# Inverting the delta rule's unit triangles: 32-blocks by substitution in place, instead of 16-blocks joined by products

## Chip, cores and metric

One core of a Trainium2 chip runs the whole kernel in one launch. The time is device microseconds of one execution. The engines are named as the profile names them: PE (TensorE, matmuls), DVE (VectorE), ACT (ScalarE), POOL (GpSimd) and SP (SyncE, which here only issues DMA transfers).

## The reference

Four layers run one after the other on 256 rows of width 1024: two attention layers, then two layers of a mixer followed by a gated feed-forward. The mixer has three branches, and one of them is the gated delta rule in chunks of 64 rows, with 4 heads:

```python
k_beta = k * beta[..., None]
m = jnp.where(strict, jnp.einsum('bhnid,bhnjd->bhnij', k_beta, k) * decay, 0.0)
a = m + jnp.eye(CHUNK, dtype=m.dtype)
rhs = jnp.concatenate([v * beta[..., None], k_beta * jnp.exp(G)[..., None]], axis=-1)
sol = lax.linalg.triangular_solve(a, rhs, left_side=True, lower=True, unit_diagonal=True)
u, w = sol[..., :dv], sol[..., dv:]
...
def step(state, inp):
    v_new = u_c - jnp.einsum('bhck,bhkv->bhcv', w_c, state)
    o = jnp.einsum('bhck,bhkv->bhcv', qd_c, state) + jnp.einsum('bhcj,bhjv->bhcv', a_c, v_new)
    state = state * dl_c[..., None, None] + jnp.einsum('bhck,bhcv->bhkv', kt_c, v_new)
```

What the change touches is the inverse of `a`, a unit lower triangle of 64 x 64 for each chunk and head (16 of them a layer).

## The kernel before

Rows lie on the 128 partitions, in two tiles `tt` of 128 rows (two chunks each). Every dense product runs on weights that are streamed in pieces: `piece` (line 423) loads a piece into a `raw` slot, ACT rounds it to `whi`, DVE forms the rest `wlo`, and `mm3` makes three matmuls of it. Between the dense products stand the small steps of attention or of the mixer.

The order is not written by hand. All operations are recorded first (`record`, line 237), with the boxes of the tiles that they read and write; overlapping boxes make dependencies. A planner (`schedule`, line 303) then goes through time with a cost for each operation and, on each engine, takes the earliest recorded one that is ready; `emit` (line 381) writes the instructions out in that order, so in the profile nearly all carry line 391. Tiles come from classes with a fixed number of slots (12 of `b`, 8 of `s`, 5 PSUM slots of `sd`, 4 of `raw`, 7 each of `whi` and `wlo`), given out in the order in which the tiles were recorded. A box is narrowed by an index only as long as the tile was not rearranged: a view made by `rearrange` keeps the whole box it had (`LA`, line 114).

The mixer (line 940) computes the strict triangle `M` per row tile and head (line 1183) and inverts `I + M` in three stages:

1. The solve (lines 1213 to 1228). `d16` masks the 16-blocks of the diagonal, a reduction packs them into `cN`, and eight small transfers bring each block into one partition of `Nb` (64 blocks on 64 partitions). Fifteen steps of a multiply and a subtract then build the inverse of each block in `Tb`. Eight transfers bring them back into `cT` (line 1231), all eight writing a rearranged view.
2. The expansion (lines 1232 to 1238): `Tm` sets the blocks on the diagonal, and DVE transposes them into `Sm`. `level4` (line 1242) joins pairs of 16-blocks to 32-blocks: per row tile four products of `M` and `Sm`, a mask, four products of `Tm` and the result, a subtraction, then small transposes into `Te`.
3. `level5` (line 1257) joins 32-blocks to 64-blocks in the same way, on 64-wide tiles.

`uu` and `wq` (line 1298) follow, then the state loop over four chunks (line 1317), the output and its branch product. In the recorded order the solve stands behind half 0 of the pool branch, and then come gate and branch products, the convolutions of v and q (`qkv`, line 1127), `vb` and `kb`; `level4` is called after half 0 of the retention branch and before `qkv(0)`, `level5` after the scores `attnT`.

Of the kernel before, what the change touches and what calls it, by code (L numbers as in the profile page):

```python
# [12 lines left out]
AF = mybir.ActivationFunctionType  # L13
ALU = mybir.AluOpType
AX = mybir.AxisListType

P = 128
S = 256
# [13 lines left out]
def rope_np(pos, dim):  # L32
    inv = np.float32(10000.0) ** (-np.arange(0, dim, 2, dtype=np.float32) / np.float32(dim))
    ang = pos.astype(np.float32)[:, None] * inv.astype(np.float32)[None, :]
    ang = np.concatenate([ang, ang], axis=-1).astype(np.float64)
    sgn = np.concatenate([-np.ones(dim // 2), np.ones(dim // 2)])
    return np.cos(ang), np.sin(ang) * sgn[None, :]


def tok(a):  # L40
    return a.reshape(2, P, -1).transpose(1, 0, 2).reshape(P, -1)


def constants():
    t = np.arange(S)
    rc, rs = rope_np(t // 64, 32)
    cc, cs = rope_np(t % 64, 32)
    cosA, sinA = np.concatenate([rc, cc], 1), np.concatenate([rs, cs], 1)
    cosB, sinB = rope_np(t, 64)
    cosC, sinC = rope_np(t, 32)  # L50
    i = np.arange(P)
    ident = np.eye(P)
    m0 = np.where(i[None, :] <= i[:, None], 0.0, -1e30)
    mT0 = np.where(i[None, :] >= i[:, None], 0.0, -1e30)
    c1 = [ident, tok(cosA), tok(sinA), tok(cosB), tok(sinB), tok(cosC), tok(sinC), m0, mT0]
    same = (i[:, None] // 64) == (i[None, :] // 64)
    lt1 = (same & (i[:, None] <= i[None, :])).astype(float)
    ls = (same & (i[:, None] > i[None, :])).astype(float)
    r0 = np.repeat((i[:, None] < 64).astype(float), P, 1)
    r1 = 1.0 - r0  # L60
    masks = [((i[:, None] // 16) == (i[None, :] // 16)).astype(float)]
    for lv in range(4, 5):
        b = 2 ** lv
        masks.append((((i[:, None] // (2 * b)) == (i[None, :] // (2 * b)))
                      & ((i[None, :] // b) % 2 == 1) & ((i[:, None] // b) % 2 == 0)).astype(float))
    cosR, sinR = rope_np(t, 128)
    eye16 = np.tile(np.eye(16).reshape(1, 256), (P, 1))
    c2 = [lt1, ls, r0, r1, lt1.T] + masks + [tok(cosR), tok(sinR), eye16]
    gam = 1.0 - 2.0 ** (-5.0 - np.arange(4))
    jj, ii = t[:, None], t[None, :]  # L70
    ex = np.where((jj // 64) == (ii // 64), np.abs(ii - jj), ii - jj)
    dd = [np.where((jj // 64) <= (ii // 64), g ** np.maximum(ex, 0).astype(float), 0.0) * 128 ** -0.5 for g in gam]
    pc = []
    for w in (2, 4, 8, 16):
        pc.append(((jj <= ii) & (jj > ii - w)) / np.minimum(ii + 1.0, w) - (jj == ii))
    d0 = np.concatenate([a[:P] for a in dd], 1)
    d1 = np.concatenate([a[P:, P:] for a in dd], 1)
    p0 = np.concatenate([a[:P, :P + 16] for a in pc], 1)
    p1 = np.concatenate([a[P:, P:] for a in pc], 1)
    f = lambda l: np.ascontiguousarray(np.concatenate(l, 1).astype(np.float32))  # L80
    return {"k1": f(c1), "k2": f(c2), "kd0": f([d0]), "kd1": f([d1]), "kp0": f([p0]), "kp1": f([p1])}
# [312 lines left out]
class Net:  # L394
# [527 lines left out]


    def setup2(self):
        k2 = self.const("kk", [P, 1664], self.I["k2"])
        m = lambda i: k2[:, i * P:i * P + P]
        self.lt1, self.ls, self.r0, self.r1, self.li, self.m16 = (m(i) for i in range(6))
        self.mask4 = m(6)
        self.cosR = k2[:, 896:1152].rearrange("p (t d) -> p t d", t=2)
        self.sinR = k2[:, 1152:1408].rearrange("p (t d) -> p t d", t=2)  # L930
        self.eye16 = k2[:, 1408:1664].rearrange("p (r c) -> p r c", r=16)
        self.ones = self.nc.tile("c", [P, P])
        self.nc.vector.memset(self.ones, 1.0)
        self.lt1r = self.nc.tile("c", [P, P], F32R)
        self.nc.scalar.copy(self.lt1r, self.lt1)
# [4 lines left out]
    def mixer(self, l, xT, rx, nxt):  # L940
        nc = self.nc
# [53 lines left out]
        for h0 in (0, 2):  # L995
            ps = self.sd([P, 2, S])
# [3 lines left out]
        ps = self.sd([P, 4, P])  # L1000
# [10 lines left out]
        for tt in range(2):  # L1011
# [12 lines left out]
            r = self.rsqrt(mv[:, :, 1], 4, 1.0, GN_EPS)  # L1024
# [12 lines left out]
        for g0 in (0, 2):  # L1037
            ps = self.sd([P, 2, S])
# [4 lines left out]
            ps = self.sd([P, 2, S])  # L1043
# [25 lines left out]
        d = sm()  # L1069
# [14 lines left out]
        ps = self.sd([P, 4, 8])  # L1084
# [25 lines left out]
        for tt in range(2):  # L1110
# [3 lines left out]
            ps = self.sd([P, 4, P])  # L1114
# [50 lines left out]
        M = em  # L1165
        bhr, bGr = nc.tile("m", [P, 8]), nc.tile("m", [P, 8])
        for tt in range(2):
            h8 = slice(tt * 4, tt * 4 + 4)
            ps = self.sd([P, 4, P])
# [9 lines left out]
            r, r2 = self.tiny(4), self.tiny(4)  # L1179
# [30 lines left out]

        y = [self.b(12 + tt, [P, D]) for tt in range(2)]
        branch("w_branch_pool_2", 0, oT, 0, gate(1, 0), True)
        cp = self.b(0, [P, 832])
        cN, cT = (cp[:, i * P:i * P + P].rearrange("p (t h c) -> p t h c", t=2, h=4) for i in range(2))
        Nb, Tb = (cp[0:64, 320 + i * 256:576 + i * 256].rearrange("p (r c) -> p r c", r=16) for i in range(2))
        for tt in range(2):
            d16 = self.s2([P, 4, P])
            nc.vector.tensor_tensor(d16, M[:, tt], self.hb(self.m16), ALU.mult)
            nc.vector.tensor_reduce(cN[:, tt], d16.rearrange("p h (b c) -> p h c b", c=16), AX.X, ALU.add)
            for h in range(4):  # L1220
                nc.sync.dma_start(Nb[(tt * 4 + h) * 8:(tt * 4 + h) * 8 + 8], cN[:, tt, h])
        nc.vector.tensor_copy(Tb, self.eye16[0:64])
        for j in range(15):
            r, c = 15 - j, j + 1
            tmp = cp[0:64, 256:256 + r * c].rearrange("p (r c) -> p r c", r=r)
            nc.vector.tensor_tensor(tmp, Nb[:, c:16, j:j + 1].to_broadcast([64, r, c]),
                                    Tb[:, j:j + 1, 0:c].to_broadcast([64, r, c]), ALU.mult)
            nc.vector.tensor_tensor(Tb[:, c:16, 0:c], Tb[:, c:16, 0:c], tmp, ALU.subtract)
        for tt in range(2):
            for h in range(4):  # L1230
                nc.sync.dma_start(cT[:, tt, h], Tb[(tt * 4 + h) * 8:(tt * 4 + h) * 8 + 8])
        Tm, Sm = self.b(8, [P, 2, 4, P]), self.b(9, [P, 2, 4, P])
        for tt in range(2):
            nc.vector.tensor_tensor(Tm[:, tt].rearrange("p h (b c) -> p h b c", c=16),
                                    cT[:, tt].unsqueeze(2).to_broadcast([P, 4, 8, 16]),
                                    self.m16.rearrange("p (b c) -> p b c", c=16).unsqueeze(1).to_broadcast([P, 4, 8, 16]),
                                    ALU.mult)
            nc.vector.transpose(Sm[:, tt].rearrange("p h d -> p (h d)"), Tm[:, tt].rearrange("p h d -> p (h d)"))

        Te = [self.s2([64, 4, 64]) for tt in range(2)]  # L1240

        def level4():
            for tt in range(2):
                ps = self.sd([P, 4, P])
                for h in range(4):
                    nc.tensor.matmul(ps[:, h], M[:, tt, h], Sm[:, tt, h], start=True, stop=True)
                wt = self.s2([P, 4, P])
                nc.vector.tensor_tensor(wt, ps, self.hb(self.mask4), ALU.mult)
                ps = self.sd([P, 4, P])
                for h in range(4):  # L1250
                    nc.tensor.matmul(ps[:, h], Tm[:, tt, h], wt[:, h], start=True, stop=True)
                nc.vector.tensor_tensor(Sm[:, tt], Sm[:, tt], ps, ALU.subtract)
                for c in (0, 32):
                    nc.vector.transpose(Te[tt][c:c + 32, :, c:c + 32], Sm[2 * c:2 * c + 32, tt, :, 2 * c:2 * c + 32])
                    nc.gpsimd.memset(Te[tt][c:c + 32, :, 32 - c:64 - c], 0.0)

        def level5():
            v = lambda t: t.rearrange("p (c o r) -> p c o r", c=2, o=2)
# [22 lines left out]
        for tt in range(2):  # L1281
            nc.vector.tensor_tensor(kb[:, tt], kn[:, tt], hd(bGr, tt), ALU.mult)
        branch("w_branch_ret_2", 0, oT, 4, gate(2, 0), False)
        level4()
        qkv(0, qT)
        rqs = []
        for tt in range(2):
# [3 lines left out]
        for tt in range(2):  # L1291
            ps = self.sd([P, 4, P])
# [7 lines left out]
        for tt in range(2):  # L1300
            ps = self.sd([P, 4, P])
# [3 lines left out]
            ps = self.sd([P, 4, P])  # L1305
# [11 lines left out]
        for tt in range(2):  # L1317
            for c in range(2):
# [3 lines left out]
                if state is not None:  # L1322
                    ps = self.sd([P, 4, P])
# [4 lines left out]
                if (tt, c) != (1, 1):  # L1328
                    ps = self.sd([P, 4, P])
# [9 lines left out]
            ps = self.sd([P, 4, P])  # L1339
# [9 lines left out]
            r = self.rsqrt(ss, 4, 1.0 / P, EPS)  # L1349
# [136 lines left out]


CONST = constants()


# [16 lines left out]
```

## Time and profile before

| | |
|---|---|
| median of 3 runs | 1184.74 us (1184.53 to 1186.55) |
| profiled execution | 1184.63 us, its span 1182.9 us |
| PE busy | 1163.6 us, 98% |
| DVE busy | 875.9 us, 74% |
| ACT busy | 652.6 us, 55% |
| the mixers' solves on DVE | from 406 and from 866 us |

In a timeline each line is a start in us, a duration in us, the engine, the operation, its output and input tiles by class, shapes, and how many like it follow one another; a bracket gives the idle time before it and what ended that. Neighbouring matmuls and DVE instructions overlap, so the distance between two starts is less than a duration. A small f32 product shows as two matmuls.

### The profile page before, as it was taken

Reading aid. Unit: us, or ns where it says so; the run is one execution under the profiler, and the core shown is the slowest. Engines: PE = TensorE matmul, PEld = TensorE weight load, DVE = VectorE, ACT = ScalarE, POOL = GpSimd, SP = SyncE. Lnnn points to the kernel's source line nnn. Section 1 sums busy time; section 2 is a strip of 40 time slices with the busy share of each in tenths; the row PEclk is TensorE's granted clock in tenths of the full one; section 3 lists DMA queues with packets and bytes.
Section 4 is the critical chain, followed back from the end, with each engine's and each line's share of the span. In section 5 each row is a group of like instructions: output and inputs, shape, how many; then the busy total and the mean of one; then the engine's idle time right before and its main releaser. Section 6 shows DMA issues by size and latency. Waiting matters only on the chain.

```text
span 1182.9 us, 17313 instructions
## 1 busy us (share of the span) xinstructions
PE 1163.6 (98%) x6316; PEld 989.3 (84%) x6316; DVE 875.9 (74%) x1570; ACT 652.6 (55%) x1210; POOL 49.3 (4%) x73
## 2 busy tenths in 40 slices
PE   8999999999999999999999999999999999999997
PEld 6888898988898888788888888898888878888886
DVE  6899889997698886776565638679797777655643
ACT  6689678964465554465454436455545446544531
POOL 1100010000001000000000000000000101000000
PEclk9999999999999999999999999999999999999999
DMA  7444335645464664346644854544754354654651
GB/s 236 142 140 150 129 123 173 200 131 173 126 213 153 204 194 136 106 160 197 212 160 140 274 185 143 171 149 163 222 188 147 107 178 142 200 192 142 216 194 36
DMA packets 64662, 196.54 MB, mean 166 GB/s; under 512 B 11201, under 2 KB 12609, under 8 KB 64577
## 3 DMA queue, kind: packets, MB, share of 16 engines
q1 hardware_dynamic: 64576, 195.44, 51.0%
q8 instruction: 49, 0.80, 0.3%
q14 instruction: 37, 0.30, 0.1%
HBM read 194.10 MB, written 1.05 MB: 165 GB/s over the span
## 4 chain that ended last, share of the span: by engine, by line
PE 91%; DVE 5%; ACT 3%; issue 1%; POOLq 0%; DVEq 0%; ACTq 0%
PE acc L391 73%; PE sd L391 18%; DVE wlo L391 2%; DVE s L391 1%; DVE b L391 1%; ACT whi L391 1%; ACT s L391 1%; ACT tg L391 1%; ACT b L391 1%; ACT xh L391 1%; DVE ty L391 0%; DVE m L391 0%; DVE xl L391 0%; DVE tg L391 0%; DVE x L391 0%
## 5 line engine op out<-in xcount | busy, mean ns | idle before, releaser
L391 DVE TENSOR_TENSOR wlo<-raw,whi 128x1024 fp32r<-128x1024 f32 (+4 forms) x380 | 427.2, 1136 | 128.1 <-ACT whi L391 125.0
L391 ACT CAST whi<-raw 128x1024 fp32r<-128x1024 f32 (+4 forms) x380 | 369.2, 982 | 195.4 <-PE acc L391 141.2
L391 PE MATMUL acc<-whi,xh 128*128 128x512 f32 (+4 forms) x1184 | 445.5, 378 | 4.6 <-ACT whi L391 1.7
L391 PE MATMUL acc<-wlo,xh 128*128 128x512 f32 (+4 forms) x1184 | 442.3, 376 | 0.5 <-DVE wlo L391 0.5
L391 PE MATMUL acc<-whi,xl 128*128 128x512 f32 (+4 forms) x1184 | 441.6, 375 | 0.0
L391 PEld LDWEIGHTS acc<-whi,xh 128*128 128x128 f32 x1184 | 223.5, 189 | 42.6 <-ACT whi L391 2.4
L391 PEld LDWEIGHTS acc<-whi,xl 128*128 128x128 f32 x1184 | 223.8, 189 | 37.1 <-issue 0.4
L391 PEld LDWEIGHTS acc<-wlo,xh 128*128 128x128 f32 x1184 | 223.9, 189 | 36.5 <-DVE wlo L391 0.7
L391 PE MATMUL acc<-whi,b 128*128 128x512 f32 x328 | 107.5, 396 | 0.8 <-ACT b L391 0.8
L391 PEld LDWEIGHTS acc<-whi,b 128*128 128x128 f32 x328 | 61.5, 188 | 15.0 <-ACT b L391 1.1
L391 PE MATMUL sd<-b,b 128*128 128x128 f32 (+3 forms) x464 | 69.8, 288 | 0.0
L391 POOL TENSOR_TENSOR ty<-ty,m 128x4 f32<-128x4 f32 (+3 forms) x34 | 33.1, 978 | 852.7 <-DVE ty L391 852.7
L391 PE MATMUL acc<-wlo,b 128*128 128x512 f32 x164 | 64.9, 396 | 0.0
L391 PEld LDWEIGHTS sd<-b,b 128*128 128x128 f32 (+2 forms) x464 | 60.6, 190 | 4.3 <-DVE b L391 1.8
L391 ACT ACTIVATE b<-sd 128x512 fp32r<-128x512 f32 (+3 forms) x44 | 23.7, 538 | 63.1 <-PE sd L391 62.4
L391 ACT ACTIVATE s<-acc,r 128x512 f32<-128x512 f32 (+3 forms) x52 | 31.2, 600 | 47.0 <-PE acc L391 44.3
L391 PE MATMUL acc<-xh,whi 128*128 128x256 f32 x192 | 54.1, 282 | 0.0
L391 PE MATMUL acc<-xh,wlo 128*128 128x256 f32 x192 | 54.1, 282 | 0.0
L391 PE MATMUL acc<-xl,whi 128*128 128x256 f32 x192 | 53.9, 281 | 0.0
L391 PE MATMUL sd<-c,s 128*128 128x128 f32 (+2 forms) x268 | 42.6, 276 | 4.4 <-DVE s L391 2.8
L391 PEld LDWEIGHTS sd<-c,s 128*128 128x128 f32 (+2 forms) x268 | 32.4, 139 | 11.9 <-ACT b L391 3.3
L391 DVE SCALAR_TENSOR_TENSOR b<-sd,b 128x512 fp32r<-128x512 f32 (+3 forms) x44 | 26.9, 616 | 18.7 <-ACT b L391 17.8
(179 smaller groups left out, 1275.6 us busy)
## 6 DMA issues: line engine op xcount, KB each, us to landing
raw<-in_wt SPq DMA_DIRECT2D x308, 512.0 KB
raw<-in_wt SPq DMA_DIRECT2D x40, 256.0 KB
raw<-in_wt SPq DMA_DIRECT2D x16, 384.0 KB
raw<-in_wt SPq DMA_DIRECT2D x8, 352.0 KB
b<-in_gains SPq DMA_DIRECT2D x5, 512.0 KB
raw<-in_wt SPq DMA_DIRECT2D x8, 264.0 KB
b<-in_kd SPq DMA_DIRECT2D x2, 512.0 KB
kk<-in_k SPq DMA_DIRECT2D x1, 832.0 KB
```

The lines of the kernel that those rows point to most:

```text
L391: o.inst = getattr(eng[o.eng], o.name)(*[real(a) for a in o.args], **{k: real(v) for k, v in o.kw.items()})
```

## The change

The diagonal blocks are now 32 wide: 32 of them, one on each of 32 partitions, each with 32 x 32 elements. The mask constants `m16`, `mask4` and `eye16` give way to one mask `m32`, and the constant tile shrinks from 1664 to 1280 columns. The substitution runs in place in `Nb`, a tile of its own, over 30 steps. `level4` is gone; `joined`, called where it was called, negates `Nb` on ACT, brings the blocks back by eight transfers, expands and transposes them, and fills `Te` by copies on ACT instead of transposes on DVE. `Sm`, `Te` and `Tm` are recorded there, later than before, and `Tm` comes from class `s` instead of `b`. The sides of the small transfers are plain slices, so that their boxes are exact.

```diff
-        cp = self.b(0, [P, 832])
-        cN, cT = (cp[:, i * P:i * P + P].rearrange("p (t h c) -> p t h c", t=2, h=4) for i in range(2))
-        Nb, Tb = (cp[0:64, 320 + i * 256:576 + i * 256].rearrange("p (r c) -> p r c", r=16) for i in range(2))
-        for tt in range(2):
-            d16 = self.s2([P, 4, P])
-            nc.vector.tensor_tensor(d16, M[:, tt], self.hb(self.m16), ALU.mult)
-            nc.vector.tensor_reduce(cN[:, tt], d16.rearrange("p h (b c) -> p h c b", c=16), AX.X, ALU.add)
-            for h in range(4):
-                nc.sync.dma_start(Nb[(tt * 4 + h) * 8:(tt * 4 + h) * 8 + 8], cN[:, tt, h])
-        nc.vector.tensor_copy(Tb, self.eye16[0:64])
-        for j in range(15):
-            r, c = 15 - j, j + 1
-            tmp = cp[0:64, 256:256 + r * c].rearrange("p (r c) -> p r c", r=r)
-            nc.vector.tensor_tensor(tmp, Nb[:, c:16, j:j + 1].to_broadcast([64, r, c]),
-                                    Tb[:, j:j + 1, 0:c].to_broadcast([64, r, c]), ALU.mult)
-            nc.vector.tensor_tensor(Tb[:, c:16, 0:c], Tb[:, c:16, 0:c], tmp, ALU.subtract)
...
-        def level4():
+        cp = self.b(0, [P, 768])
+        cN, cT = (cp[:, i * S:i * S + S].rearrange("p (t h c) -> p t h c", t=2, h=4) for i in range(2))
+        Nb = self.b(0, [32, 32, 32])
+        for tt in range(2):
+            d32 = self.s2([P, 4, P])
+            nc.vector.tensor_tensor(d32, M[:, tt], self.hb(self.m32), ALU.mult)
+            nc.vector.tensor_reduce(cN[:, tt], d32.rearrange("p h (b c) -> p h c b", c=32), AX.X, ALU.add)
+            for h in range(4):
+                nc.sync.dma_start(Nb[(tt * 4 + h) * 4:(tt * 4 + h) * 4 + 4], cp[:, (tt * 4 + h) * 32:(tt * 4 + h) * 32 + 32])
+        nc.gpsimd.memset(Nb.rearrange("p r c -> p (r c)")[:, 0:1024:33], -1.0)
+        for j in range(1, 31):
+            r, c = 31 - j, j + 1
+            tmp = cp[0:32, 512:512 + r * j].rearrange("p (r c) -> p r c", r=r)
+            nc.vector.tensor_tensor(tmp, Nb[:, c:32, j:c].to_broadcast([32, r, j]),
+                                    Nb[:, j:c, 0:j].to_broadcast([32, r, j]), ALU.mult)
+            nc.vector.tensor_tensor(Nb[:, c:32, 0:j], Nb[:, c:32, 0:j], tmp, ALU.subtract)
+        def joined():
+            nc.scalar.activation(Nb, Nb, AF.Copy, scale=-1.0)
             for tt in range(2):
-                ps = self.sd([P, 4, P])
                 for h in range(4):
-                    nc.tensor.matmul(ps[:, h], M[:, tt, h], Sm[:, tt, h], start=True, stop=True)
-                wt = self.s2([P, 4, P])
-                nc.vector.tensor_tensor(wt, ps, self.hb(self.mask4), ALU.mult)
-                ps = self.sd([P, 4, P])
-                for h in range(4):
-                    nc.tensor.matmul(ps[:, h], Tm[:, tt, h], wt[:, h], start=True, stop=True)
-                nc.vector.tensor_tensor(Sm[:, tt], Sm[:, tt], ps, ALU.subtract)
+                    nc.sync.dma_start(cp[:, S + (tt * 4 + h) * 32:S + (tt * 4 + h) * 32 + 32],
+                                      Nb[(tt * 4 + h) * 4:(tt * 4 + h) * 4 + 4])
+            Sm = self.b(9, [P, 2, 4, P])
+            Te = [self.s2([64, 4, 64]) for tt in range(2)]
+            for tt in range(2):
+                Tm = self.s2([P, 4, P])
+                nc.vector.tensor_tensor(Tm.rearrange("p h (b c) -> p h b c", c=32),
+                                        cT[:, tt].unsqueeze(2).to_broadcast([P, 4, 4, 32]),
+                                        self.m32.rearrange("p (b c) -> p b c", c=32).unsqueeze(1).to_broadcast([P, 4, 4, 32]),
+                                        ALU.mult)
+                nc.vector.transpose(Sm[:, tt].rearrange("p h d -> p (h d)"), Tm.rearrange("p h d -> p (h d)"))
                 for c in (0, 32):
-                    nc.vector.transpose(Te[tt][c:c + 32, :, c:c + 32], Sm[2 * c:2 * c + 32, tt, :, 2 * c:2 * c + 32])
+                    nc.scalar.copy(Te[tt][c:c + 32, :, c:c + 32], cT[2 * c:2 * c + 32, tt])
                     nc.gpsimd.memset(Te[tt][c:c + 32, :, 32 - c:64 - c], 0.0)
+            return Sm, Te
...
         branch("w_branch_ret_2", 0, oT, 4, gate(2, 0), False)
-        level4()
+        Sm, Te = joined()
         qkv(0, qT)
```

## Rows read from the trace of the kernel before

**Rows 1.** The page, parts 1 and 4: busy time by engine, and the last chain.

```profile
PE 1163.6 (98%) x6316; PEld 989.3 (84%) x6316; DVE 875.9 (74%) x1570; ACT 652.6 (55%) x1210; POOL 49.3 (4%) x73
...
PE 91%; DVE 5%; ACT 3%; issue 1%; POOLq 0%; DVEq 0%; ACTq 0%
```

**Rows 2.** Timeline of PE, two of its waits late in the mixers.

```profile
489.06 0.50 PE L391 MATMUL acc<-whi,b 128*128 128x512 f32 x1 [0.82 <-ACT b L391]
...
956.19 0.47 PE L391 MATMUL acc<-whi,xh 128*128 128x512 f32 x1 [0.79 <-DVE tg L391]
```

**Rows 3.** Timeline of PE around `level4`, both layers.

```profile
455.31 2.05 PE L391 MATMUL sd<-b,b 128*128 128x128 f32 x16
457.11 0.48 PE L391 MATMUL acc<-wlo,xh 128*128 128x512 f32 x1
...
457.86 1.95 PE L391 MATMUL sd<-s,b 128*128 128x128 f32 x16
459.65 0.60 PE L391 MATMUL sd<-c,b 128*128 128x128 f32 x4
...
914.47 1.95 PE L391 MATMUL sd<-b,b 128*128 128x128 f32 x16
916.26 0.60 PE L391 MATMUL sd<-c,b 128*128 128x128 f32 x4
```

**Rows 4.** Timeline of DVE, layer one, from the solve to the join.

```profile
406.11 0.59 DVE L391 TENSOR_TENSOR b<-b 64x15 f32<-64x15 f32 x3
...
413.48 0.21 DVE L391 TENSOR_TENSOR b<-b 64x60 f32<-64x60 f32 x1
413.61 0.67 DVE L391 SCALAR_TENSOR_TENSOR tg<-tg,acc 128x512 f32<-128x512 f32 x1
...
421.24 1.80 DVE L391 TENSOR_TENSOR b<-b 64x55 f32<-64x55 f32 x8
422.98 1.23 DVE L391 TENSOR_TENSOR wlo<-raw,whi 128x1024 fp32r<-128x1024 f32 x1
424.12 0.36 DVE L391 TENSOR_TENSOR b<-b 64x15 f32<-64x15 f32 x2
...
453.34 1.28 DVE L391 TENSOR_TENSOR b<-b,kk 128x512 f32<-128x512 f32 x2
...
455.77 1.25 DVE L391 TENSOR_TENSOR b<-sd,m 128x512 f32<-128x512 f32 x2
...
459.26 0.68 DVE L391 TENSOR_TENSOR b<-b,sd 128x512 f32<-128x512 f32 x1
...
461.06 0.61 DVE L391 STREAM_TRANSPOSE s<-b 32x128 f32<-32x128 f32 x2
```

**Rows 5.** Timelines of SP and DVE: small transfers, second reduction, last transfer's use.

```profile
375.84 0.79 SPq L391 DMA_DIRECT2D b<-b  x1
...
401.27 0.62 SPq L391 DMA_DIRECT2D b<-b  x1
...
390.40 1.03 DVE L391 TENSOR_REDUCE b<-s 128x64 f32<-128x512 f32 x1
...
907.72 0.63 SPq L391 DMA_DIRECT2D b<-b  x1
...
911.70 0.69 DVE L391 TENSOR_TENSOR b<-b,kk 128x512 f32<-128x512 f32 x1 [3.18 <-DMA raw<-in_wt]
```

**Rows 6.** Windows: length, then busy us (instructions) of PE, PEld, DVE, ACT, POOL.

```profile
389.00:440.00 51.00, 51.00 (x312) 45.52 (x311) 44.18 (x86) 26.62 (x36) 0.00 (x0) 1.00 0.60 193
440.00:453.00 13.00, 13.00 (x57) 10.52 (x56) 6.94 (x9) 4.87 (x6) 0.00 (x0) 1.00 0.71 216
```

**Rows 7.** Timeline of ACT, one cast of the stretch, with its wait.

```profile
414.87 1.05 ACT L391 CAST whi<-raw 128x1024 fp32r<-128x1024 f32 x1 [2.56 <-PE acc L391]
```

**Rows 8.** Timeline of PE: `level5` begins, `uu` begins.

```profile
461.97 0.68 PE L391 MATMUL sd<-b,s 128*64 128x64 f32 x8
...
467.41 4.82 PE L391 MATMUL sd<-b,b 128*128 128x128 f32 x40
```

More of the change, by code (lines that the diff above doesn't have):

```diff
@@ L60, in constants @@
     r1 = 1.0 - r0
[L61 to L65, printed above, removed]
+    m32 = ((i[:, None] // 32) == (i[None, :] // 32)).astype(float)
     cosR, sinR = rope_np(t, 128)
-    eye16 = np.tile(np.eye(16).reshape(1, 256), (P, 1))
-    c2 = [lt1, ls, r0, r1, lt1.T] + masks + [tok(cosR), tok(sinR), eye16]
+    c2 = [lt1, ls, r0, r1, lt1.T, m32, tok(cosR), tok(sinR)]
     gam = 1.0 - 2.0 ** (-5.0 - np.arange(4))
@@ L924, in setup2 @@
     def setup2(self):
-        k2 = self.const("kk", [P, 1664], self.I["k2"])
+        k2 = self.const("kk", [P, 1280], self.I["k2"])
         m = lambda i: k2[:, i * P:i * P + P]
[L927 to L931, printed above, removed]
+        self.lt1, self.ls, self.r0, self.r1, self.li, self.m32 = (m(i) for i in range(6))
+        self.cosR = k2[:, 768:1024].rearrange("p (t d) -> p t d", t=2)
+        self.sinR = k2[:, 1024:1280].rearrange("p (t d) -> p t d", t=2)
         self.ones = self.nc.tile("c", [P, P])
@@ L1229, in mixer @@
-        for tt in range(2):
-            for h in range(4):
[L1231 to L1238, printed above, removed]
@@ L1240, in mixer @@
-        Te = [self.s2([64, 4, 64]) for tt in range(2)]
-        def level4():
+                nc.sync.dma_start(Nb[(tt * 4 + h) * 4:(tt * 4 + h) * 4 + 4], cp[:, (tt * 4 + h) * 32:(tt * 4 + h) * 32 + 32])
[6 more added lines that the diff above has]
+            nc.vector.tensor_tensor(Nb[:, c:32, 0:j], Nb[:, c:32, 0:j], tmp, ALU.subtract)
```

## The prediction, made before the changed kernel ran

> **What bounds the kernel now.** I read the page first: TensorE is busy 98% of the span, and the chain of work that ended last is TensorE for 91% [rows 1]. So a change pays only if TensorE gets less to do or waits less, and it costs only if it makes TensorE wait. Then I listed, in the timeline of TensorE, every wait of it. Inside the two mixers they come late: 0.82 us at 489.06 for the split of the delta-rule output, and 0.79 us at 956.19 at the same place of layer two [rows 2]. That is where the dense work that TensorE can do meanwhile (the last gate) has run out. So the mixer has two lengths that are nearly equal: TensorE's own work, and a chain of dependent steps: the triangular solve on DVE, its eight transfers home, level 4, level 5, the products `uu`, the state loop, the output. The change shortens the first and alters the second; both are worked out, and the longer one decides. I take layer one's stamps; layer two repeats them some 459 us later.
>
> **Removed from TensorE.** Level 4 is two steps of eight f32 products (each appears as two matmuls, hence x16). The bars overlap, so I price a step by when the next matmul starts: 457.11 - 455.31 = 1.80 us, 459.65 - 457.86 = 1.79 us; layer two's first step is 916.26 - 914.47 = 1.79 us, and I count its second alike [rows 3]. Four steps: 7.2 us. TensorE was not waiting around them, and the change gives it nothing new. If TensorE stays the longer of the two lengths, all of it is gained.
>
> **The solve on DVE.** Before: 15 steps of two instructions, 2 x 680 = 1360 elements a partition. After: 30 steps, j = 1 to 30, each with j(31 - j) elements twice: 60 instructions and 9920 elements. Prices: 0.68 us at 512 elements (459.26) and 0.21 us at 60 (413.48) give 0.47/452 = 1.04 ns an element. Behind the one with 60 elements independent work starts 0.13 us later; 0.06 of it are elements, so the fixed part is 0.07 us. In a run of eight with nothing between (340 elements), 421.24 to 422.98, the fixed part is (1.74 - 0.35)/8 = 0.175 us [rows 4]. So the new solve occupies between 60 x 0.07 + 10.3 = 14.5 us (other work between all of them) and 60 x 0.175 + 10.3 = 20.8 us (none); the old one 3.5 to 6.7 us. I take the low end, because between 406 and 424 most neighbours were other instructions. The trace shows no 32-partition form with these strides; I price it by elements, as 128- and 64-partition rows go.
> [...]
>
> **When the solve starts.** Of the eight transfers out, the first is issued at 375.84 and the last at 401.27, and the first multiply starts at 406.11 [rows 4, 5]. The planner saw the destination of each as the whole of one region and so spaced them out. With exact boxes each group of four can be issued back to back. The second reduction must still wait for the first four, since `cN` keeps its whole box. By rows: four issues of about 0.65 us, 4.0 us from an issue to the use of its data (907.72 to 911.70), the reduction 1.03 us, four more issues, 4.0 us: 375.8 + 2.0 + 4.0 + 1.0 + 1.9 + 4.0 = 389 [rows 5]. The -1 on the diagonal is one POOL memset of 32 elements behind the last transfer; POOL is busy 4% of the span [rows 1]. Bounds: 389 if nothing comes between, 406 if weight loads on SP's queue hold the transfers as they do now.
>
> **When it ends.** Solve instructions were recorded before the later weights, so the planner takes one whenever its predecessor is done and fills the pauses with others. The old solve needed 424.12 + 0.36 - 406.11 = 18.4 us for 30 instructions, 1.4 of it elements: 0.57 us each, the others' turns included [rows 4]. At that pace the new one needs 60 x 0.57 + 10.3 = 44.3 us and ends at 433. Check by capacity: from 389 to 440 DVE is busy 44.2 of 51 us [rows 6]; less the old solve (about 5.4) and the second reduction (1.0), plus the `vb` scaling (1.25) that gets its buffer earlier, 39.0 remain. So 12.0 us are free where 14.5 are needed: 2.5 us of other work slide past 440, where 6.1 of 13 us are free. What slides is mostly `wlo` and the convolution of q. `wlo` runs ahead of TensorE: ScalarE's cast before it waits for a slot that TensorE frees [rows 7]. So TensorE doesn't see the delay. Worst case: the solve gets free time alone, and ends between 445 and 453.
>
> **From the solve to `uu`.** After: the negation on ScalarE, 1024 elements, 1.05 us as for a cast of that width [rows 7] and some 0.3 of hand-over; then eight transfers, 7 x 0.63 and 4.0 us for the last: 9.7 us. Behind the first, SP's weight loads wait; up to 3 us for loads in between. So the expansion (`Tm`) starts at 443 to 446. From there three pairs of 512-wide DVE instructions, 1.25 us a pair as the `vb` pair at 455.77: `kb` if it comes first, the expansions, the transposes. Then level 5 to `uu` as now, 467.41 - 461.97 = 5.4 us: 9.2 us in all. Before: from 453.34 to 467.41, 14.1 us, level 4 inside it [rows 4, 8]. `uu` thus starts at 452 to 455 instead of 467.4: the chain is 12 us or more earlier, more than the 3.6 us by which TensorE is relieved. TensorE decides.
> The new waits have queues behind them. ScalarE's negation waits for the whole solve, and casts `whi` stand behind it. The transfers home, recorded later than now, come on SP's queue behind the loads of gate and branch recorded before them, which are issued earlier in any case, and loads behind them wait for the negation. Both kinds run ahead by the slots that they fill; a negation late by a microsecond or two costs nothing while that lead holds.
>
> **Other parts, at nothing.** DVE loses level 4's two masks, two subtractions and four small transposes, 2 x 0.6 + 2 x 0.6 + 4 x 0.3 = 3.6 us a layer [rows 4]; ScalarE gains four copies of 128 elements, each an eighth of a cast's, and is busy 55% of the span [rows 1]. `Sm` is now recorded after `vb` and `kb`, so `vb` gets a buffer before the solve ends and frees two PSUM slots; the transposes of q and the scores can move ahead of the join. That moves work within TensorE and adds none. If this cover were gone (q late by the sliding work), the price is the chain's, below. The constants shrink by 192 KB, loaded long before.
>
> **Sum.** The profiled execution took 1184.63 us (span 1182.9, so 1.7 around it), 0.1 below the median of the three, so the sum needs no shift. -7.2 for level 4, and of the waits -0.8, the one at 489.06: with the chain 12 us ahead, the gate is no longer used up before it. The wait at 956.19 sits behind the last product and stays. 1184.63 - 7.2 - 0.8 = 1176.6. If the other goes too, and another as large of layer one's tail, 1175.0.
>
> **Rivals.** First, slower: the solve ends late and the chain becomes the bound. The place is the join; TensorE then waits between 487 and 497 with no gate left. The point from which it decides: `uu` at 467.4 means `Tm` at 458.2 and the end of the solve at about 446.5. If the start stays at 406, the solve ends at 450.4, `Tm` starts near 461.8, `uu` at 471.0, 3.6 us later; with no spare dense work each layer loses that: 1184.6 + 7.2 = 1191.8. For it: DVE is 87% busy from 389 to 440, SP does hold transfers behind weight loads. Against: the planner gives the solve precedence, and 13 us lie between 433 and the point. Chance 0.18. With 20.8 us, the price without any overlap, the solve would need more than the 12.0 + 6.1 us free before 453, and this would be the outcome. [...]
> Second, the change buys nothing: the solve ends between 443 and 448, what level 4 freed turns into waiting, and the time stays within 2.4 us of 1184.6. The exact boxes not speeding the start, as the second reduction still waits, leads here too with a faster pace. Chance 0.13.
> Third, partly: the chain binds in one layer only, 1184.6 - 3.6 = 1181.0. Chance 0.07.
>
> **How the numbers follow.** The forecast, 1176.6, has 0.62. Faster by over 0.2% (2.4 us, about what a measurement of this kernel can tell) is forecast and third rival: 0.69. Same 0.13, slower 0.18. The range goes from 1174.0 (all waits gone, and 1 us for a reshuffled order, which moves either way) up to 1187.0, through the no-change case and into the weak end of the slower one; it leaves out about 0.16 above and 0.04 below.
>
> **What would show it.** Right: no 128x128 x16 pairs ahead of level 5; the eight transfers out within about 13 us, the solve starting near 389 and ending before 442; `Tm` before 455; TensorE without new waits around 460 to 500. Wrong in the chain: a wait of TensorE for a DVE or ScalarE result there, longer than 0.8 us. Wrong in the cover: waits of accumulating matmuls for `wlo` between 390 and 455. Wrong in the price: 240-element multiplies well over 0.4 us long.

## The result and the profile after

The changed kernel takes 1172.97 us (median of four, 1172.51 to 1173.46) where the kernel before takes 1184.63 beside it: the ratio is 0.9898, interval 0.9881 to 0.9916, 11.7 us less. Two more measurements on other chips gave 0.9911 (0.9896 to 0.9926) and 0.9905 (0.9890 to 0.9920). The forecast was 1176.6 in a range from 1174.0 to 1187.0: the direction was right, the gain was 8.0 where 11.7 came, and the range ended 1.0 us too high.

The page of the changed kernel, parts 1 and 4, to lay beside [rows 1]:

```profile
PE 1154.4 (99%) x6252; PEld 981.2 (84%) x6252; DVE 887.4 (76%) x1612; ACT 655.6 (56%) x1220; POOL 50.3 (4%) x75
...
PE 89%; DVE 6%; ACT 3%; DMA 1%; issue 1%; SPq 0%; POOLq 0%; DVEq 0%; ACTq 0%
```

TensorE has 64 matmuls less, which is level 4 in both layers (4 steps of 16), and is 9.2 us less busy; the span fell by 11.2 us, from 1182.9 to 1171.7. So some 2 us of the gain are idle time, and the bars shrank by 2 us more than the products' 7.2; as bars overlap (2.05 us long for 1.80 from start to start in [rows 3]), their sum is no price, and the distances between starts below are. DVE is busier by 11.5 us, and TensorE does not wait for it in the changed part.

The timelines of SP and DVE after, layer one, to lay beside [rows 4, 5]: the transfers out, the first step, a step in the middle, the last, then the join.

```profile
376.06 2.57 SPq L386 DMA_DIRECT2D b<-b  x4
...
380.43 1.07 DVE L386 TENSOR_REDUCE b<-s 128x128 f32<-128x512 f32 x1
...
381.53 2.57 SPq L386 DMA_DIRECT2D b<-b  x4
...
389.09 0.19 DVE L386 TENSOR_TENSOR b<-b 32x30 f32<-32x30 f32 x1
...
408.61 0.39 DVE L386 TENSOR_TENSOR b<-b 32x240 f32<-32x240 f32 x1
408.93 0.46 DVE L386 SCALAR_TENSOR_TENSOR s<-s,pp,s 128x253 f32<-128x253 f32 x1
...
436.20 0.17 DVE L386 TENSOR_TENSOR b<-b,b 32x30 f32<-32x30 f32 x1
...
437.55 5.30 SPq L386 DMA_DIRECT2D b<-b  x8
...
446.31 1.28 DVE L386 TENSOR_TENSOR s<-b,kk 128x512 f32<-128x512 f32 x2
```

The solve starts at 389.09 and ends at 436.4; an instruction of 240 elements is 0.39 us long and lets the next, independent one start 0.32 us after it. Behind 46 of the 60 instructions another one stands before the solve goes on. `Tm` starts at 446.31, which was 453.34 before.

TensorE after, layer one, to lay beside [rows 3, 8]: level 5 in two groups, then `uu`.

```profile
448.81 1.15 PE L386 MATMUL sd<-b,s 128*64 128x64 f32 x16
...
451.12 1.11 PE L386 MATMUL sd<-s,s 64*64 64x64 f32 x16
...
453.44 4.82 PE L386 MATMUL sd<-b,b 128*128 128x128 f32 x40
```

`uu` starts 14.0 us earlier than before (467.41). The timeline shows no wait of TensorE in either mixer behind its beginning any more; those of [rows 2] are gone, and two in layer one that I had left aside. What they cost shows in the distances between starts. The kernel before, timeline of TensorE around these waits:

```profile
487.65 0.60 PE L391 MATMUL sd<-c,b 128*128 128x128 f32 x4
...
494.52 0.60 PE L391 MATMUL sd<-c,b 128*128 128x128 f32 x4
494.88 0.47 PE L391 MATMUL acc<-whi,b 128*128 128x512 f32 x1
495.69 0.66 PE L391 MATMUL sd<-c,b 128*128 128x128 f32 x4 [0.33 <-DVE b L391]
497.22 0.47 PE L391 MATMUL acc<-whi,xh 128*128 128x512 f32 x1 [0.88 <-DVE tg L391]
...
954.74 0.66 PE L391 MATMUL sd<-c,b 128*128 128x128 f32 x4
```

Up to the starts in [rows 2], the group at 487.65 takes 1.41 us and the one at 954.74 takes 1.45; the matmul at 494.88 takes 0.81 and the group at 495.69 takes 1.53. Such a group without a wait takes 0.36 us (494.52 to 494.88), such a matmul behind one 0.32. So the waits cost 1.05 + 0.49 + 1.17 + 1.09 = 3.8 us, where the gaps in the brackets add up to 2.8. Summed over both stretches of the next section, the steps from start to start of these two kinds of matmul (`sd<-c,b` and `acc<-whi,b`) are 3.5 us shorter after the change. The chain of work that ended last, in the same stretch after (start, length, whose work), has nothing of another engine in it:

```profile
475.47 0.46 PE sd L386 x4
475.93 4.19 PE acc L386 x18
480.12 0.44 PE sd L386 x4
480.56 9.78 PE acc L386 x42
490.33 0.44 PE sd L386 x4
490.77 3.25 PE acc L386 x14
```

The transposes of both row tiles' outputs (475.47, 480.12) are now done while the last gate's products still run.

### The profile page after: what moved, and what is told of

It reads as the page before. It is cut to its first block, busy times and chain, and to the rows that moved or that the text cites. A ratio compares the mean times of both kernels' runs of the same rounds, so it can differ in the third digit from the quotient of the medians.

```text
span 1171.7 us, 17240 instructions
## 1 busy us (share of the span) xinstructions
PE 1154.4 (99%) x6252; PEld 981.2 (84%) x6252; DVE 887.4 (76%) x1612; ACT 655.6 (56%) x1220; POOL 50.3 (4%) x75
## 3 DMA queue, kind: packets, MB, share of 16 engines
HBM read 193.90 MB, written 1.05 MB: 166 GB/s over the span
## 4 chain that ended last, share of the span: by engine, by line
PE 89%; DVE 6%; ACT 3%; DMA 1%; issue 1%; SPq 0%; POOLq 0%; DVEq 0%; ACTq 0%
PE acc L386 71%; PE sd L386 17%; DVE wlo L386 2%; DVE b L386 2%; DVE s L386 2%; ACT whi L386 1%; ACT s L386 1%; ACT tg L386 1%; DMA raw<-in_wt 0%; ACT b L386 0%; ACT xh L386 0%; DMA gc<-in_gcol 0%; DMA b<-b 0%; DVE ty L386 0%; SPq L386 0%
## 5 line engine op out<-in xcount | busy, mean ns | idle before, releaser
L386 PE MATMUL sd<-b,b 128*128 128x128 f32 (+4 forms) x432 | 66.2, 289 | 0.0
L386 PEld LDWEIGHTS sd<-b,b 128*128 128x128 f32 (+2 forms) x432 | 56.9, 190 | 3.9 <-DVE b L386 1.3
L386 PEld LDWEIGHTS sd<-c,s 128*128 128x128 f32 (+2 forms) x268 | 32.2, 138 | 11.7 <-ACT b L386 3.3
```

The lines of the kernel that those rows point to most:

```text
L386: o.inst = getattr(eng[o.eng], o.name)(*[real(a) for a in o.args], **{k: real(v) for k, v in o.kw.items()})
```

## The experiments

The start of the program varies by up to 2.5 us between profiles (the first wait of mixer one ends between 359.9 and 362.3), ahead of all that is changed here. So beside the ratios I compare two stretches: from the first wait of mixer one to the same wait of mixer two, and from there to the end of the span. For the kernel before these marks are

```profile
362.12 0.71 PE L391 MATMUL sd<-b 128*128 128x128 f32 x4 [0.44 <-DVE b L391]
...
821.75 0.71 PE L391 MATMUL sd<-b 128*128 128x128 f32 x4 [0.34 <-DVE b L391]
```

and for the changed kernel

```profile
362.28 0.71 PE L386 MATMUL sd<-b 128*128 128x128 f32 x4 [0.48 <-DVE b L386]
...
815.23 0.71 PE L386 MATMUL sd<-b 128*128 128x128 f32 x4 [0.36 <-DVE b L386]
```

Each ratio is to the kernel before on the same chip; its medians there were 1184.63, 1183.64, 1183.37 and 1183.48 us, so the medians of different chips compare less closely than the ratios.

| kernel | median us | ratio to before (interval) | stretch 1 | stretch 2 |
|---|---|---|---|---|
| before | 1184.63 | 1 | 459.63 | 361.15 |
| changed | 1172.97 | 0.9898 (0.9881 to 0.9916) | 452.95 | 356.47 |
| changed, second chip | 1172.68 | 0.9911 (0.9896 to 0.9926) | 454.86 | 356.11 |
| changed, third chip | 1173.08 | 0.9905 (0.9890 to 0.9920) | 453.17 | 356.14 |
| a_products | 1181.18 | 0.9977 (0.9967 to 0.9986) | 459.42 | 360.06 |
| b_boxes | 1181.48 | 0.9977 (0.9966 to 0.9988) | 457.14 | 360.56 |
| i_boxes_no_level4 | 1175.29 | 0.9925 (0.9913 to 0.9937) | 454.53 | 356.99 |
| g_no_level4 | 1174.95 | 0.9920 (0.9906 to 0.9935) | 454.16 | 356.95 |
| c_out_whole | 1199.92 | 1.0134 (1.0117 to 1.0150) | 465.28 | 368.32 |
| d_back_whole | 1200.29 | 1.0140 (1.0124 to 1.0156) | 468.04 | 369.98 |
| e_neg4 | 1178.97 | 0.9952 (0.9934 to 0.9970) | 459.76 | 357.35 |
| e_neg8 | 1175.79 | 0.9936 (0.9921 to 0.9951) | 455.79 | 357.40 |
| j_issue650 | 1174.42 | 0.9918 (0.9905 to 0.9932) | 453.81 | 357.16 |

**What the products cost.** Level 4's number of products goes back in, with nothing hanging on them:

```diff
         Sm, Te = joined()
+        for tt in (0, 1, 0, 1):
+            ps = self.sd([P, 4, P])
+            for h in range(4):
+                nc.tensor.matmul(ps[:, h], M[:, tt, h], M[:, tt, h], start=True, stop=True)
```

> The changed kernel with level 4's number of products put back where it was called (16 f32 products of 128x128 a layer, M by M, results unread). Theory 1: the products cost 7.2 us and the rest of the gain (11.7 - 7.2 = 4.5 us) is waiting of TensorE that went because the chain to uu ends earlier; so about 1173.0 + 7.2 = 1180.2, with TensorE still without waits in the mixers. Theory 2: the products cost more than their spacing shows (changes between f32 and dense products) and the whole gain is theirs: 1183 to 1184.6.

1181.18. From start to start the products put back take 3.48 us in the first layer and 3.49 in the second, by the trace, near the 3.59 read from [rows 3] for two steps. The second stretch is longer by as much, 360.06 - 356.47 = 3.59 us. The first is 6.5 us longer; part of the rest are waits of another order that the changed kernel does not have, this one in its timeline of TensorE and another of 0.72 us at 744.22:

```profile
446.16 0.68 PE L386 MATMUL sd<-b,s 128*64 128x64 f32 x8 [0.96 <-ACT s L386]
```

Theory 1 stands in the price: the products are some 7 us, not the whole gain. Its "without waits" did not come.

**What the earlier chain gives by itself.** The kernel before, level 4 included, with plain slices on both sides of its small transfers:

```diff
-                nc.sync.dma_start(Nb[(tt * 4 + h) * 8:(tt * 4 + h) * 8 + 8], cN[:, tt, h])
+                k = tt * 4 + h
+                nc.sync.dma_start(cp[k * 8:k * 8 + 8, 320:576].rearrange("p (r c) -> p r c", r=16), cp[:, k * 16:k * 16 + 16])
...
-                nc.sync.dma_start(cT[:, tt, h], Tb[(tt * 4 + h) * 8:(tt * 4 + h) * 8 + 8])
+                nc.sync.dma_start(cp[:, P + k * 16:P + k * 16 + 16], cp[k * 8:k * 8 + 8, 576:832].rearrange("p (r c) -> p r c", r=16))
```

> The kernel before with exact boxes for its sixteen small transfers and nothing else; level 4 stays. Theory 1: solve and join come some 15 us or more earlier, the four waits late in the mixers go; priced by starts and not by bars they are 0.97 + 0.58 + 1.09 us in layer one and 1.0 us in layer two, 3.6 us: 1181.0. My prediction's own view, that only the wait at 489 goes: 1183.8. Theory 2: 1184.6, no change, as no product is removed.

1181.48, interval of the gain 1.4 to 4.0 us; by the marks 2.5 us in the first stretch and 0.6 in the second. `uu` starts at 453.41, as in the changed kernel, and the late waits are gone:

```profile
453.41 4.82 PE L391 MATMUL sd<-b,b 128*128 128x128 f32 x40
```

So no product need go for the waits to go, and more goes than the 0.8 us of my prediction. The steps priced above are 3.6 us shorter in its trace, as expected; the two stretches together are 3.1 us shorter, as other steps and the end of the program took 0.5 us back.

**The changed kernel's products without its solve.** The kernel b_boxes with level 4 left out (the join of 16-blocks is not computed; the 16-block solve stays):

```diff
-                    nc.tensor.matmul(ps[:, h], M[:, tt, h], Sm[:, tt, h], start=True, stop=True)
...
-                    nc.tensor.matmul(ps[:, h], Tm[:, tt, h], wt[:, h], start=True, stop=True)
-                nc.vector.tensor_tensor(Sm[:, tt], Sm[:, tt], ps, ALU.subtract)
```

> The kernel before with exact boxes and with level 4 left out (the join of 16-blocks is not computed): TensorE's products are those of the changed kernel, the solve stays the short one on 16-blocks. Theory 1 (the whole gain is the four product steps and the waits that the earlier chain removes; the longer solve costs nothing): within 1.5 us of the changed kernel. Theory 2 (the longer solve on DVE costs something that is hidden in the sum): 2 us or more faster than the changed kernel.

1175.29, and 2.2 us slower than the changed kernel beside it (1173.08), where I had allowed for faster; the intervals of the two ratios overlap a little. Both theories missed the sign. TensorE has the same 6252 matmuls and one short wait in its mixers (0.33 us at 419.34), but is busy 1156.7 us instead of 1154.6. A part shows in the groups of level 5, matmuls by form; first this kernel, then the changed one:

```profile
L391 PE MATMUL sd<-s,s 64*64 64x64 f32 x32 | 3.1, 227 | 0.0
L391 PE MATMUL sd<-b,s 128*64 128x64 f32 x32 | 2.7, 228 | 0.0
```

```profile
L386 PE MATMUL sd<-b,s 128*64 128x64 f32 x32 | 2.3, 225 | 0.0
L386 PE MATMUL sd<-s,s 64*64 64x64 f32 x32 | 2.3, 220 | 0.0
```

Equal counts, and bars of 5.8 us against 4.6; from start to start, which leaves out what overlaps, 5.1 us against 4.3. Here eight or fewer stand in a row, there sixteen. The other small products `sd<-b,b` take 0.7 us more here by the same count, and the matmuls around the wait at 419.34 take 0.6 more: together 2.1 of the 2.2 us. That the order of the small products is the cause is read from the traces, not tried by itself. The longer solve on DVE costs TensorE nothing that these runs can find.

**Level 4 left out, whole boxes kept.** The same cut from the kernel before:

> The kernel before with level 4 left out (products, masks, subtractions; the join of 16-blocks is not computed), everything else as before, whole boxes included. Theory 1: 7.2 us of products, and a chain about 6 us shorter against 3.6 us less dense cover, so 2.4 us of waiting a layer at most goes: 1.0 to 3.4 us more; 1174 to 1176.5. Theory 2, the whole gain of the change is the products': 1173.

1174.95, 8.7 us less than before on its chip (1183.64): 7.2 for the products and, by subtraction, 1.5 of the waits. As the chain is only some 6 us shorter here, this wait remains, and one as long at 946.08 in layer two (timeline of TensorE):

```profile
491.06 0.47 PE L391 MATMUL acc<-whi,xh 128*128 128x512 f32 x1 [0.43 <-DVE tg L391]
```

**The slower rival, made to happen.** The changed kernel with whole boxes again, on the way out or on the way home:

```diff
+        Nw = Nb.rearrange("p (r a) c -> p r (a c)", a=1)
-                nc.sync.dma_start(Nb[(tt * 4 + h) * 4:(tt * 4 + h) * 4 + 4], cp[:, (tt * 4 + h) * 32:(tt * 4 + h) * 32 + 32])
+                nc.sync.dma_start(Nw[(tt * 4 + h) * 4:(tt * 4 + h) * 4 + 4], cN[:, tt, h])
```

> The changed kernel with whole boxes for the eight transfers out (back stays exact). The solve should start near 406 as in the kernel before, and end near 450. My prediction's slower rival: 1191.8. Theory 1 with the chain as measured now (uu at 453.5 in layer one, some 14 us later here, of which about 7.7 us are covered by dense work left over): 6 us a layer, about 1185 to 1186, with TensorE waiting between 480 and 500. Theory 2, the chain plays no part: 1173.

1199.92. Solve, join and `uu` by the timelines of DVE, SP and PE:

```profile
409.50 0.19 DVE L386 TENSOR_TENSOR b<-b 32x30 f32<-32x30 f32 x1
...
458.38 0.18 DVE L386 TENSOR_TENSOR b<-b,b 32x30 f32<-32x30 f32 x1
...
473.01 6.53 PE L386 MATMUL sd<-b,b 128*128 128x128 f32 x40 [0.29 <-DVE b L386]
...
492.99 0.63 PE L386 MATMUL sd<-c,b 128*128 128x128 f32 x4 [1.83 <-DVE b L386]
```

The solve starts at 409.5 and needs 49 us, so it ends at 458.6, past the 446.5 that the prediction named as the point of decision, and `uu` starts 19.6 us later than in the changed kernel. That layer got 12.3 us longer, part of it at a lower clock, so at least 7.3 us were covered; 7.7 were supposed. The time is 14 us above what I expected here and 8 above the rival's price, for two reasons that the trace shows: the solve ended 8 us later than at the old pace, and once TensorE waited, the clock granted to it fell (last section; 0.982 to 0.988 in the mean of its executions, where the kernel before on that chip has 0.994 to 0.998).

```diff
-                    nc.sync.dma_start(cp[:, S + (tt * 4 + h) * 32:S + (tt * 4 + h) * 32 + 32],
+                    nc.sync.dma_start(cT[:, tt, h],
```

> The changed kernel with whole boxes for the eight transfers home (out stays exact). Planned one behind the other, some 2.9 us apart instead of 0.65: the last is issued about 16 us later. Theory 1: 7 us covered, 9 us a layer or more not (the granted clock fell in out_whole when TensorE waited): 18 to 26 us more, 1191 to 1199. Theory 2, exact boxes matter on the way out alone, as weight loads stand between there: no change.

1200.29. The eight transfers home go out one by one from 435.11 to 460.49 instead of in 5.3 us, and `uu` starts at 471.04:

```profile
435.11 0.63 SPq L386 DMA_DIRECT2D b<-b  x1
...
471.04 4.89 PE L386 MATMUL sd<-b,b 128*128 128x128 f32 x40 [0.34 <-DVE b L386]
```

So exact boxes matter on either way. Without one of them this change is 1.3 to 1.4% slower than the kernel before.

**How much slack the chain has.** More negations ahead of the transfers home, in an even number:

```diff
-            nc.scalar.activation(Nb, Nb, AF.Copy, scale=-1.0)
+            for _ in range(5):
+                nc.scalar.activation(Nb, Nb, AF.Copy, scale=-1.0)
```

> The changed kernel with four more negations of the blocks on ScalarE ahead of the transfers home (1.05 us each and a hand-over): the chain to uu is 4.8 us longer in each layer, TensorE's work is the same. Theory 1 (TensorE decides, the chain has slack): out_whole moved uu from 453.4 to 473.0 in layer one, 19.6 us, and that layer got 12.3 us longer, so about 7 us are covered; 4.8 us cost nothing, within 1 us of the changed kernel. Theory 2 (the chain still decides): 2 x 4.8 = 9.6 us more.

> The same with eight more negations, 9.6 us in each layer. Theory 1: 7 us of it covered, 2 to 3 us a layer not, so 4 to 6 us more than the changed kernel, with the waits between the output of the first and the second row tile and behind it back. Theory 2: 19 us more.

The changed kernel beside them:

> The changed kernel again, on the chip of the next three, for comparison: 1.0% below the kernel before (ratio 0.988 to 0.992).

It took 1172.68; with eight more negations (9 in all) the time is 1175.79, 3.1 us more, near the 4 to 6 of theory 1 and far from 19. One of the late waits is back, 0.88 us at 946.88 in layer two, and a few of 0.2 to 0.3 us in layer one. Four more gave 1178.97, 6.3 us more where I expected nothing. That result is a miss of theory 1, and no run here shows four negations without the wait that follows. It is not the chain's length, since twice as much cost half. The timelines of TensorE and of DVE show where:

```profile
451.69 0.68 PE L386 MATMUL sd<-b,s 128*64 128x64 f32 x8 [1.85 <-DVE b L386]
```

```profile
450.33 0.69 DVE L386 TENSOR_TENSOR s<-b,kk 128x512 f32<-128x512 f32 x1 [2.12 <-DMA b<-b]
```

The plan had level 5 at a point where the last block was not home yet: DVE waited 2.12 us for the transfer and TensorE 1.85 us for DVE, with dense work behind this step in the plan's order; in layer two the same place has a wait of 0.79 us at 909.49. The expensive part came after, in the granted clock (last section).

**A planner that knows the transfers.** Issue and landing of a small transfer set to 650 and 2500 ns in the planner instead of 460 and 1500:

```diff
-                hw = max(hw, t) + 460
+                hop = bool(o.outs and o.ins)
+                if hop:
+                    now[e] = t + 650.0
+                hw = max(hw, t) + (650 if hop else 460)
...
-                o.end = dma + (3500 if o.cost > 500 else 1500)
+                o.end = dma + (3500 if o.cost > 500 else 2500 if hop else 1500)
```

> The changed kernel with the planner told what the trace shows of a small transfer: 0.65 us from issue to issue and 4.0 us from issue to use, where it assumed 0.46 and 2.8. In neg4 and in one profile of the changed kernel TensorE stood at level 5 for 1.1 to 1.9 us, since the plan had the blocks home earlier than they were. Theory 1: level 5 is planned behind more dense work, that wait cannot come, 0 to 1.5 us faster than the changed kernel. Theory 2: another order of equal worth, within 1 us.

> The changed kernel a third time, beside the next two on one chip: ratio 0.989 to 0.992.

1174.42 beside 1173.08: no better. It has no wait at level 5, and puts level 5 in groups of eight again: its two stretches are together 1.7 us longer than the changed kernel's beside it, 0.6 of it in level 5 from start to start. No run here beats the changed kernel.

## Why the prediction was wrong

Most of its steps came as worked out. **Level 4's price** of 7.2 us holds: as many products cost 3.48 and 3.49 us a layer in a_products. **The price of the solve** holds: 0.39 us for 240 elements and the next, independent instruction 0.32 us behind its start, mostly between other instructions. **Its start**, 389 by the sum of rows, was 389.09; **its end**, 433, was 436.4, 47 us for 44. The hand-over around the negation, an estimate of 0.3 us, was 0.1: the last step's bar ends at 436.37, the negation's runs from 436.46 to 437.52 and the first transfer home is issued at 437.55. **`Tm`**, 443 to 446, was 446.3; **`uu`**, 452 to 455, was 453.4. **TensorE decides**, and the cover held: no accumulating matmul waited for `wlo` in the stretch where DVE was fullest.

The step that failed is **the sum**, in its second term. I credited 0.8 us of waiting, the bar's gap at 489.06, and wrote that the wait at 956.19 "sits behind the last product and stays". Measured from start to start, 3.5 us of waiting went, and b_boxes, with no product removed, loses 3.6 us of it and all of the late waits. Three readings were wrong. My list of "every wait" priced none of the two at 495.69 and 497.22. The wait at 956.19 is not "at the same place" as the one at 489.06: it is the twin of 497.22 (both wait for `tg` of DVE), and 489.06 has no twin in layer two. And this pair is not a fixed tail: it is there because the second row tile's output comes when the last gate's products are used up. With the chain 14 us earlier its transposes come at 480, and the gate's products run on until 484. Besides, the gap between two bars is not the price of a wait, since the bars of matmuls reach past the point where the next can start (dense ones are 0.39 us long and 0.23 apart).

1184.6 - 7.2 - 3.5 is 1173.9, and 1 us is left. By the trace it lies in the order of the small products, which I had put at nothing ("moves work within TensorE and adds none"), with 1 us either way in the range: level 5's 64 matmuls take 4.3 us from start to start instead of 4.9, now that sixteen stand in a row, and the products `sd<-b,b` outside level 4 take about 0.5 us less. i_boxes_no_level4 and j_issue650, which have level 5 in eights, are slower than the changed kernel beside them; no run changes that order alone, so this microsecond is read and not shown, and which order the planner comes to is luck as far as my prediction goes.

Of the **rivals**, the slower one had the right mechanism: c_out_whole drove the solve's end past 446.5 and the kernel lost. Its price was too low (1191.8 for 1199.9), it left out the clock, and the waits began at 471.6 already, not at 487. The second and third rival, a gain eaten by waiting in both layers or in one, did not come: no wait stands in either join of the profile above. On the second chip one of 1.10 us does (last section), with a median no longer for it (1172.68).

## What to carry to other kernels

If removed work and a shortened chain meet in one change, list every wait of the bounding engine in every layer, price each from start to start, less what the same step takes without a wait, and ask of each whether dense work left over could fill it; a tail is a tail only if no work is left. A list planner's dependencies are part of the kernel's speed: here with the longer solve, views that kept their whole box on one way of the transfers cost 27 us (1199.9 and 1200.3 against 1173). Test a removal by putting the work back without its dependencies, and by taking the dependencies alone.

## What the runs showed of the hardware

A short wait of TensorE cost more than itself in e_neg4. It waited 1.85 us at 451.69; the windows after it (length, busy us of PE, granted clock, DMA share, GB/s):

```profile
448.00:452.00 4.00, 2.15 (x14) 1.00 0.52 141
452.00:456.00 4.00, 4.00 (x26) 0.54 0.22 47
456.00:460.00 4.00, 4.00 (x18) 0.50 0.23 90
460.00:464.00 4.00, 4.00 (x27) 0.68 0.72 251
464.00:468.00 4.00, 4.00 (x26) 1.00 0.62 206
```

For some ten microseconds TensorE, busy throughout, had about half its clock (0.54, 0.50 and 0.68 in the rows): 4 x (0.46 + 0.50 + 0.32) = 5.1 us of full-clock work lost by this estimate, more than the wait. Three of its four executions took 1178.9 to 1179.2 us at a mean clock of 0.993 or 0.994, the fourth 1175.2 at 0.996; so the loss seems not to come in full each time. In c_out_whole, after a wait of 1.84 us, the clock was 0.70 in the four microseconds behind 472, and 0.89 on average from 475 to 500. After the waits of 0.8 to 0.9 us in the kernel before, and after one of 1.10 us in the changed kernel on its second chip,

```profile
452.97 1.11 PE L386 MATMUL sd<-s,s 64*64 64x64 f32 x16 [1.10 <-ACT s L386]
```

it stayed at 1.00. But the length of one wait does not settle it: in layer two of c_out_whole the clock was 0.50 from 952 to 964 behind four waits of 0.68 to 0.85 us between 943 and 952, none of them long. In these runs a wait placed by a slip of the plan was thus a risk of another size than its length. It is not what sets orders of equal work apart here: in the first stretch the clock was 1.00 throughout in the changed kernel, i_boxes_no_level4 and j_issue650.
